# Encoder layer on one core: constant tables of the mixers loaded and split later, and the first k-tiles of the first gate block loaded singly

## The chip, the core and the metric

The kernel runs on one core of a Trainium2 chip. The metric is device time in microseconds (us). TensorE (PE in the rows) does the matmuls, ScalarE (ACT) and VectorE (DVE) the elementwise work, SyncE (SP) issues nearly all loads, and GpSimd (POOL) issues a few loads that add on the way.

## The reference

One layer, 256 tokens of 2048 numbers, all in fp32 (norms and rotations cut):

```
h = x + 0.5 * rms(swiglu(rms(x, g1)), p1)                 # first feed-forward step
u = rms(h, g);  q, k, v, f, g = split(u @ w_in)           # 16 query heads, 4 key/value heads
y_attn = gqa(rotate(rms(q)), rotate(rms(k)), v) @ w_attn_o
y_four = real(fft2(f, axes=(positions, 128 channels of a group))) @ w_fourier
h = h + rms((sigmoid(gA + bA) * y_attn + sigmoid(gB + bB) * y_four) @ w_out, p)
y = h + 0.5 * rms(swiglu(rms(h, g2)), p2)                 # second feed-forward step
```

## The kernel before

Each fp32 product is three matmuls of rounded numbers (`mm3`, L110 to L112): high part by high part, the same left side by the low part, low part by high part. `split` (L104, L105) makes the parts: ACT copies a tile into the high part (`whi`, `uh`), DVE subtracts that from the tile to get the low part (`wlo`, `ul`). In the rows `whi`, `wlo` are parts of weights, `raw` is the weight tile as loaded. Weights come through SP in 512 KB loads of two k-tiles into a ring of five raw tiles, and their parts go into a ring of six. `wk` is a pool of eight small tiles, `xpool` one of three larger ones. One 512-column `mm3` for each of the two token tiles and each of 16 k-tiles makes a block of 512 output columns (`col_block`, matmuls named `pc`).

Program order on each engine comes from a scheduler that keeps to dependences and resources; `tc.issue_after(x)` adds that an instruction stands behind x on its engine, and `latest["V"]` is the DVE instruction of the last `split`. `last_rows` is an exception: there DVE's order is written out by hand.

The places that the steps below touch, in order of time:

- `gate0` (L776 to L791): the first gate block of the first feed-forward step. For k-tiles 0 and 1 one weight tile (256 KB) and one tile of the input (`xt`, 128.5 KB) each, after that pairs (512 KB, 257 KB). `uh` (L786) and `ul` are the scaled input's parts.
- The end of the first feed-forward step and the start of the mixers (`last_rows`): DVE adds the normed result to h (L405), multiplies h by the next norm's gain (y, L418), and TensorE turns that (`pt`, L180) for the next input's parts. The constants' loads and splits are written at the start of the mixers: gains `gq`, `gk`, rotation tables `rc`, `rsn`, then the six tables of the discrete Fourier transform: `dps`, `dcs` (with low parts), `odd`, `first`, `alt`, `mid` (high part alone); their raw tiles are named `draw` and `mraw`.
- Gates 10 to 13 with `fold_f` between: the Fourier branch's product with its weight tile `fraw`, whose matmuls are named `pe`. `turn_k` transposes keys (`kT`) in gate 12.
- Gate 6 (j=0 of the attention loop) with `fourier_positions` (`pa`; `zh`, `zl` are the parts of `zs`; `al`, `ol` the low parts of its results, L973ff) and `fourier_channels` (`pb`, L1003ff) between its k-tiles.
- `fourier_weights(cb)` (L1107 to L1128): for each of four pieces of `w_fo` one load, two DVE steps in place (L1118, L1119), a `split`, and an accumulation (`acc`, L1126, L1128). `fourier_out(cb)` (L1133ff) uses them, in matmuls named `pf`; it is written behind the gate and `attn_scores` (`sc`, row maximum `mx`, exponentials `p`).

Of the kernel before, what the change touches and what calls it, by code (L numbers as in the profile page):

```python
# [2 lines left out]

# [1 line left out]

# [5 lines left out]
F32 = mybir.dt.float32  # L11
F32R = mybir.dt.float32r
BF16 = mybir.dt.bfloat16
I32 = mybir.dt.int32
AF = mybir.ActivationFunctionType
# [3 lines left out]
P = 128  # L19
# [39 lines left out]
def encoder_layer(  # L59
# [24 lines left out]
    def load(dst, src):  # L84
        nc.sync.dma_start(dst, src)
# [4 lines left out]
    def work(name, shape=None):  # L90
        return wk.tile(shape or [P, NB], F32, tag="wk", name=name)
# [11 lines left out]
    def split(hi, lo, src):  # L103
        a = A.activation(hi, src, AF.Copy)  # L104
        v = V.tensor_tensor(out=lo, in0=src, in1=hi.bitcast(F32), op=ALU.subtract)  # L105
        latest["A"], latest["V"] = a.ins, v.ins
# [83 lines left out]
    def col_block(u, w, nb, between=(), at=()):  # L190


        at = list(at)
        ps = [pmm.tile([P, NB], F32, tag="mm", name="pc") for _ in range(NT)]
        step = KD / (len(between) + 1)
        done = 0
        for kg in range(KD // CK):
            wt = weights(w[nb, kg])
            for k in range(CK):
                kk = kg * CK + k  # L200
                while at and kk >= at[0][0]:
                    with tc.issue_after(mm.ins):
                        at.pop(0)[1]()
                if done < len(between) and kk >= (done + 1) * step:
                    if between[done]:
                        with tc.issue_after(mm.ins):
                            between[done]()
                    done += 1
                for t in range(NT):
                    mm = mm3(ps[t][:], u[t][0][:, kk, :], u[t][1][:, kk, :], *wt[k], kk == 0, kk == KD - 1)  # L210
        return ps
# [563 lines left out]

    def gate0():  # L776
        ps = [pmm.tile([P, NB], F32, tag="mm", name="pc") for _ in range(NT)]
        for kk, n in [(0, 1), (1, 1)] + [(k, 2) for k in range(2, KD, 2)]:
            wt = piece(f1_gate[0, kk // CK], kk % CK, n)
            xt = xpool.tile([P, 2, S + 1], F32, tag="xt", name="xt")[:, 0:n, :]  # L780
            load(xt, xgT[:, kk:kk + n, :])
            xv = xt[:, :, 0:S].rearrange("p k (t c) -> p k t c", t=NT)
            for k in range(n):
                for t in range(NT):
                    uh, ul = u[t][0][:, kk + k, :], u[t][1][:, kk + k, :]
                    A.activation(uh, xv[:, k, t, :], AF.Copy, scale=xt[:, k, S:S + 1])  # L786
                    V.scalar_tensor_tensor(out=ul, in0=xv[:, k, t, :], scalar=xt[:, k, S:S + 1],
                                           in1=uh.bitcast(F32), op0=ALU.mult, op1=ALU.subtract)
                    mm3(ps[t][:], uh, ul, *wt[k], kk + k == 0, kk + k == KD - 1)
            if kk == 8:  # L790
                load(ident[:], ident_in)  # L791
        return ps
# [28 lines left out]
        load(spill[t], h[t][:])  # L821

    gq, gk = work("gq", [P, HD]), work("gk", [P, HD])
    load(gq[:], q_g.partition_broadcast(P))
    load(gk[:], k_g.partition_broadcast(P))
    rc, rsn = work("rc", [P, NT, HD]), work("rsn", [P, NT, HD])
    load(rc[:], rope_cos)
    load(rsn[:], rope_sin)
    tabs = {}

    def tables():
        for nm, g in (("q", gq), ("k", gk)):
# [59 lines left out]
        ts = slice(t * P, (t + 1) * P)  # L892
        transpose4(kro[t], kT[:, 0, :, ts], kT[:, 1, :, ts])

    def constant(src, n):
        raw = work("draw", [P, n])
        load(raw[:], src)
        return raw

    WE, WO = P + 2, P  # L900
    dps = const.tile([P, 2, WE + WO], F32R, name="dps")
    split(dps[:, 0, :], dps[:, 1, :], constant(dft_pos, WE + WO)[:])
    dcs = const.tile([P, 2, 2 * P], F32R, name="dcs")
    split(dcs[:, 0, :], dcs[:, 1, :], constant(dft_ch, 2 * P)[:])
    odd = const.tile([P, WE], F32R, name="odd")
    A.activation(odd[:], constant(dft_ones[:, 0:WE], WE)[:], AF.Copy)
    first = const.tile([P, P], F32R, name="first")
    A.activation(first[:], constant(dft_ones[:, WE:WE + P], P)[:], AF.Copy)
    alt = xpool.tile([P, GROUPS // 2, NYR], F32R, tag="xt", name="alt")
    A.activation(alt[:].rearrange("p a b -> p (a b)"), constant(dft_ones[:, WE + P:], GROUPS // 2 * NYR)[:], AF.Copy)  # L910
    mid = xpool.tile([NS, 2 * P + 2 * NYR], F32R, tag="xt", name="mid")
    mraw = work("mraw", [NS, 2 * P + 2 * NYR])
    load(mraw[:], dft_mid)
    A.activation(mid[:], mraw[:], AF.Copy)


    fs, fraw = [], {}
# [80 lines left out]
    def fourier_channels(b, i, a):  # L998

        (ah, al), (oh, ol) = a  # L1000
        j = 2 * b + i
        if j == 0:
            foT.append(new_chunk("foT"))
            pmid[0] = ptr.tile([P, NB], F32, tag="tr", name="pn")
        pb = ptr.tile([P, NB], F32, tag="tr", name="pb")
        c = slice(i * WO, (i + 1) * WO)
        mm3(pb[:, 0:WO], dcs[0:PO, 0, P:2 * P], dcs[0:PO, 1, P:2 * P], oh[0:PO, c], ol[0:PO, c], True, True)
        c, m, o = slice(i * WE, (i + 1) * WE), slice(2 * WE, 3 * WE), pb[:, WO:WO + WE]
        mm3(o, dcs[0:PO, 0, 0:P], dcs[0:PO, 1, 0:P], ah[0:PO, c], al[0:PO, c], True, False)
        T.matmul(o, mid[:, i * P:(i + 1) * P], ah[0:NS, m], start=False, stop=False)  # L1010
        T.matmul(o, mid[:, i * P:(i + 1) * P], al[0:NS, m], start=False, stop=True)
        o = pmid[0][0:NYR, 0:WE]
        T.matmul(o, alt[0:PO, j, :], ah[0:PO, c], start=j == 0, stop=False)
        T.matmul(o, alt[0:PO, j, :], al[0:PO, c], start=False, stop=False)
        if i == 1:
            n = slice(2 * P + b * NYR, 2 * P + (b + 1) * NYR)
            T.matmul(o, mid[:, n], ah[0:NS, m], start=False, stop=False)
            T.matmul(o, mid[:, n], al[0:NS, m], start=False, stop=b == 1)
        split(foT[0][0][:, j, :], foT[0][1][:, j, :], pb[:, 0:2 * P])
        A.activation(dcol[:, j:j + 1], pb[:, 2 * P:2 * P + 1], AF.Copy)  # L1020
        if j == 3:
            A.activation(mids[0:NYR, :], pmid[0][0:NYR, 0:P], AF.Copy)
            V.tensor_tensor(out=mids[64:NYR, :], in0=pmid[0][64:NYR, 0:P], in1=mids[64:NYR, :].bitcast(F32), op=ALU.subtract)
            A.activation(dcol[0:GROUPS, 4:5], pmid[0][0:GROUPS, P:P + 1], AF.Copy)
# [81 lines left out]
    def fourier_weights(cb):  # L1106


        acc = xpool.tile([P, NB], F32, tag="xt", name="acc")
        nraw, wn = xpool.tile([P, NB], F32, tag="xt", name="nraw"), workr("wn")  # L1110
        load(nraw[0:NYR, :], w_fn[cb])
        A.activation(wn[0:NYR, :], nraw[0:NYR, :], AF.Copy)
        V.tensor_tensor(out=wn[32:40, :], in0=nraw[32:40, :], in1=wn[32:40, :].bitcast(F32), op=ALU.subtract)
        forms = []
        for j in range(4):
            raw = wraw.tile([P, 2, NB], F32, tag="raw", name="raw")
            load(raw[:], w_fo[cb, j].rearrange("p (k c) -> p k c", k=2))
            V.tensor_tensor(out=raw[:, 0, :], in0=raw[:, 0, :], in1=raw[:, 1, :], op=ALU.add)  # L1118
            V.scalar_tensor_tensor(out=raw[:, 1, :], in0=raw[:, 1, :], scalar=-2.0, in1=raw[:, 0, :],  # L1119
                                   op0=ALU.mult, op1=ALU.add)  # L1120
            hi = wring.tile([P, 2, NB], F32R, tag="hi", name="whi")
            lo = wring.tile([P, 2, NB], F32R, tag="lo", name="wlo")
            split(hi[:], lo[:], raw[:])
            forms.append((hi, lo))
            if j == 0:
                V.tensor_scalar(out=acc[:], in0=raw[:, 0, :], scalar1=dcol[:, j:j + 1], scalar2=None, op0=ALU.mult)  # L1126
            else:
                V.scalar_tensor_tensor(out=acc[:], in0=raw[:, 0, :], scalar=dcol[:, j:j + 1], in1=acc[:],  # L1128
                                       op0=ALU.mult, op1=ALU.add)
        ready[cb] = acc, nraw, wn, forms  # L1130
# [21 lines left out]
            V.tensor_tensor(out=cbs(mB[t], cb), in0=w[:], in1=cbs(mB[t], cb), op=ALU.mult)  # L1152


    pv = col_block(u, w_in, 5, between=[nxt.finish, tables, lambda: fold_tokens(0)])
    for t in range(NT):
        vt = work("vt")
        A.activation(vt[:], pv[t][:], AF.Copy, scale=rs[t][:, 0:1])
# [7 lines left out]
    pq = col_block(u, w_in, 0, at=folds_at(4))  # L1166
    qs = []
    gate(11, mB, 1, at=folds_at(4), between=[lambda t=t: qs.append(norm_rope(pq, "q", t)) for t in range(NT)])
    gate(12, mB, 2, at=folds_at(4), between=[lambda t=t: turn_k(t) for t in range(NT)])
    gate(13, mB, 3, at=folds_at(4))  # L1170

    yA, zA = ([big(f"{n}{t}") for t in range(NT)] for n in ("yA", "zA"))
    mT = []
# [210 lines left out]
```

## Time and profile before

| | us |
|---|---|
| median of 3 runs (lowest, highest) | 2004.93 (2003.99, 2006.01) |
| profiled execution | 2006.3 |
| its span, first to last instruction | 2004.2 |
| TensorE busy, of that span | 1984.0 |
| VectorE busy | 1780.1 |
| ScalarE busy | 1301.2 |

The profiled execution has its own time beside its span: 2.1 us lie around the span, and the execution is 1.4 us above the median. Times in the rows are counted from the span's start. The mean granted TensorE clock is 0.997 of full speed.

### The profile page before, as it was taken

Reading aid. Unit: us, or ns where it says so; the run is one execution under the profiler, and the core shown is the slowest. Engines: PE = TensorE matmul, PEld = TensorE weight load, DVE = VectorE, ACT = ScalarE, POOL = GpSimd, SP = SyncE. Lnnn points to the kernel's source line nnn. Section 1 sums busy time; section 2 is a strip of 40 time slices with the busy share of each in tenths; the row PEclk is TensorE's granted clock in tenths of the full one; section 3 lists DMA queues with packets and bytes.
Section 4 is the critical chain, followed back from the end, with each engine's and each line's share of the span. In section 5 each row is a group of like instructions: output and inputs, shape, how many; then the busy total and the mean of one; then the engine's idle time right before and its main releaser. Section 6 shows DMA issues by size and latency. Waiting matters only on the chain.

```text
span 2004.2 us, 25805 instructions
## 1 busy us (share of the span) xinstructions
PE 1984.0 (99%) x9146; PEld 1644.8 (82%) x9146; DVE 1780.1 (89%) x2352; ACT 1301.2 (65%) x1860; POOL 84.5 (4%) x94
## 2 busy tenths in 40 slices
PE   9999999999999999999999999999999999999998
PEld 7888888888888878888888888878888888888886
DVE  6899999999999878886877885878999999999996
ACT  7566766767667756556666564656677766677666
POOL 0000000000000000100000000000000000000002
PEclk9999999999999999999999999999999999999999
DMA  8657766677668796954555557565577766677673
GB/s 319 211 175 240 225 232 199 200 249 228 226 204 275 250 280 201 261 184 138 195 189 188 192 166 277 194 215 194 169 236 231 231 210 208 213 233 229 208 264 126
DMA packets 117585, 434.20 MB, mean 217 GB/s; under 512 B 12840, under 2 KB 18992, under 8 KB 106064
## 3 DMA queue, kind: packets, MB, share of 16 engines
q1 hardware_dynamic: 103888, 411.65, 59.9%
q0 software_dynamic: 13568, 20.91, 6.0%
q8 instruction: 71, 1.16, 0.2%
q14 instruction: 58, 0.48, 0.1%
HBM read 409.44 MB, written 6.29 MB: 207 GB/s over the span
## 4 chain that ended last, share of the span: by engine, by line
PE 90%; DVE 5%; DMA 3%; ACT 1%; issue 1%; SPq 0%; DVEq 0%; ACTq 0%
PE pc L111 18%; PE pc L112 18%; PE pc L110 18%; PE pr L112 10%; PE pr L111 10%; PE pr L110 10%; DVE wlo L105 2%; PE pt L180 1%; DMA raw<-in_f_gu 1%; DMA raw<-in_w_fo 1%; DVE t L582 0%; PE pe L110 0%; PE pe L112 0%; PE pe L111 0%; PE pt L1072 0%
## 5 line engine op out<-in xcount | busy, mean ns | idle before, releaser
L105 DVE TENSOR_TENSOR wlo<-raw,whi 128x1024 fp32r<-128x1024 f32 (+1 forms) x567 | 681.1, 1219 | 96.9 <-ACT whi L104 95.2
L104 ACT ACTIVATE whi<-raw 128x1024 fp32r<-128x1024 f32 (+1 forms) x567 | 585.8, 1052 | 253.7 <-PE pc L112 109.3
L111 PE MATMUL pc<-wlo,fh 128*128 128x512 f32 x738 | 287.3, 389 | 0.0
L112 PE MATMUL pc<-whi,fl 128*128 128x512 f32 x738 | 287.3, 389 | 0.0
L110 PE MATMUL pc<-whi,fh 128*128 128x512 f32 x738 | 287.1, 389 | 0.0
L110 PE MATMUL pc<-whi,uh 128*128 128x512 f32 x688 | 271.7, 395 | 1.5 <-ACT uh L786 1.5
L111 PE MATMUL pc<-wlo,uh 128*128 128x512 f32 x688 | 269.8, 392 | 1.7 <-DVE wlo L105 1.7
L112 PE MATMUL pc<-whi,ul 128*128 128x512 f32 x688 | 269.6, 392 | 0.0
L104 ACT ACTIVATE whi<-t 128x1024 fp32r<-128x1024 f32 (+1 forms) x198 | 171.6, 867 | 139.4 <-DVE t L582 130.8
L582 DVE TENSOR_TENSOR t<-raw 128x512 f32<-128x512 f32 (+1 forms) x252 | 209.1, 842 | 14.1 <-DMA raw<-in_f_gu 10.3
L110 PE MATMUL pr<-whi,hTh 128*128 128x512 f32 x544 | 213.4, 392 | 0.0
L112 PE MATMUL pr<-whi,hTl 128*128 128x512 f32 x544 | 211.8, 389 | 0.0
L111 PE MATMUL pr<-wlo,hTh 128*128 128x512 f32 x544 | 211.7, 389 | 0.0
L105 DVE TENSOR_TENSOR wlo<-t,whi 128x1024 fp32r<-128x1024 f32 (+1 forms) x198 | 193.6, 978 | 13.4 <-ACT whi L104 13.0
L104 ACT ACTIVATE w<-raw 128x1024 fp32r<-128x1024 f32 x144 | 152.0, 1055 | 40.8 <-DVE raw L582 34.7
L105 DVE TENSOR_TENSOR w<-raw,w 128x1024 fp32r<-128x1024 f32 x144 | 175.6, 1219 | 0.0
L111 PEld LDWEIGHTS pc<-wlo,fh 128*128 128x128 f32 x738 | 138.5, 188 | 29.2 <-DVE wlo L105 0.3
L110 PEld LDWEIGHTS pc<-whi,fh 128*128 128x128 f32 x738 | 138.5, 188 | 28.9
L112 PEld LDWEIGHTS pc<-whi,fl 128*128 128x128 f32 x738 | 138.5, 188 | 28.7
L111 PEld LDWEIGHTS pc<-wlo,uh 128*128 128x128 f32 x688 | 129.8, 189 | 28.5 <-DVE wlo L105 3.6
L110 PEld LDWEIGHTS pc<-whi,uh 128*128 128x128 f32 x688 | 129.7, 188 | 28.5 <-ACT uh L786 2.8
L112 PEld LDWEIGHTS pc<-whi,ul 128*128 128x128 f32 x688 | 129.6, 188 | 27.0
(360 smaller groups left out, 3188.4 us busy)
## 6 DMA issues: line engine op xcount, KB each, us to landing
raw<-in_f_down SPq DMA_DIRECT2D x176, 512.0 KB, 5.0
raw<-in_f_gu SPq DMA_DIRECT2D x144, 512.0 KB, 4.8
raw<-in_f_gu SPq DMA_DIRECT2D x72, 1024.0 KB, 7.0
raw<-in_w_in SPq DMA_DIRECT2D x112, 512.0 KB, 4.5
raw<-in_f_up SPq DMA_DIRECT2D x32, 512.0 KB, 4.5
raw<-in_w_ao SPq DMA_DIRECT2D x32, 512.0 KB, 3.8
raw<-in_w_out SPq DMA_DIRECT2D x32, 512.0 KB, 4.5
raw<-in_f_gate SPq DMA_DIRECT2D x31, 512.0 KB, 5.8
```

The source lines that it names most:

```text
L104: a = A.activation(hi, src, AF.Copy)
L105: v = V.tensor_tensor(out=lo, in0=src, in1=hi.bitcast(F32), op=ALU.subtract)
L110: T.matmul(ps, lh, rh, start=first, stop=False, skip_group_check=onto)
L111: T.matmul(ps, lh, rl, start=False, stop=False, skip_group_check=onto)
L112: return T.matmul(ps, ll, rh, start=False, stop=last, skip_group_check=onto)
L180: T.transpose(pt[:, j, :], src[:, j * P:(j + 1) * P], ident[:])
L582: V.tensor_tensor(out=out, in0=a, in1=b, op=ALU.subtract)
```

## The change

Four edits. (1) In `gate0` the first `CK` = 4 k-tiles come singly, instead of the first two, and their input tiles move from `xpool` to `wk`. (2) The loads of `gq`, `gk`, `rc`, `rsn` become a step `rotation`, done between the k-tiles of the first column block of the mixers, and `tables`, which uses them, goes from the second slot to the fifth. (3) The six tables' loads (`ask`) and splits (`take`) go into gates 12 and 13. (4) In `fourier_weights` the first add of the first piece is put behind the last `split` on DVE.

```diff
     def gate0():
-        for kk, n in [(0, 1), (1, 1)] + [(k, 2) for k in range(2, KD, 2)]:
+        for kk, n in [(k, 1) for k in range(CK)] + [(k, 2) for k in range(CK, KD, 2)]:
             wt = piece(f1_gate[0, kk // CK], kk % CK, n)
-            xt = xpool.tile([P, 2, S + 1], F32, tag="xt", name="xt")[:, 0:n, :]
+            xt = work("xt", [P, 1, S + 1])[:] if n == 1 else xpool.tile([P, 2, S + 1], F32, tag="xt", name="xt")[:]
...
-    load(gq[:], q_g.partition_broadcast(P))
-    load(gk[:], k_g.partition_broadcast(P))
-    load(rc[:], rope_cos)
-    load(rsn[:], rope_sin)
+    def rotation():
+        load(gq[:], q_g.partition_broadcast(P))
+        load(gk[:], k_g.partition_broadcast(P))
+        load(rc[:], rope_cos)
+        load(rsn[:], rope_sin)
...
-    split(dps[:, 0, :], dps[:, 1, :], constant(dft_pos, WE + WO)[:])
-    split(dcs[:, 0, :], dcs[:, 1, :], constant(dft_ch, 2 * P)[:])
-    A.activation(odd[:], constant(dft_ones[:, 0:WE], WE)[:], AF.Copy)
-    A.activation(first[:], constant(dft_ones[:, WE:WE + P], P)[:], AF.Copy)
-    A.activation(alt[:].rearrange("p a b -> p (a b)"), constant(dft_ones[:, WE + P:], GROUPS // 2 * NYR)[:], AF.Copy)
-    load(mraw[:], dft_mid)
-    A.activation(mid[:], mraw[:], AF.Copy)
+    def ask(*names):
+        for n in names:
+            raw = work("draw", list(srcs[n].shape))
+            load(raw[:], srcs[n])
+            late[n] = raw
+    def take(*names):
+        for n in names:
+            raw = late[n]
+            if n in ("dps", "dcs"):
+                dst = {"dps": dps, "dcs": dcs}[n]
+                split(dst[:, 0, :], dst[:, 1, :], raw[:])
+            elif n in ("odd", "first"):
+                A.activation({"odd": odd, "first": first}[n][:], raw[:], AF.Copy)
...
     def fourier_weights(cb):
-            V.tensor_tensor(out=raw[:, 0, :], in0=raw[:, 0, :], in1=raw[:, 1, :], op=ALU.add)
+            with tc.issue_after(latest["V"]) if cb == 0 and j == 0 else nullcontext():
+                V.tensor_tensor(out=raw[:, 0, :], in0=raw[:, 0, :], in1=raw[:, 1, :], op=ALU.add)
...
-    pv = col_block(u, w_in, 5, between=[nxt.finish, tables, lambda: fold_tokens(0)])
+    pv = col_block(u, w_in, 5, between=[nxt.finish, rotation, lambda: fold_tokens(0), None, tables])
...
-    gate(12, mB, 2, at=folds_at(4), between=[lambda t=t: turn_k(t) for t in range(NT)])
-    gate(13, mB, 3, at=folds_at(4))
+    gate(12, mB, 2, at=folds_at(4), between=[lambda t=t: turn_k(t) for t in range(NT)]
+         + [lambda: ask("alt", "mid", "first"), None, lambda: take("alt", "mid", "first")])
+    gate(13, mB, 3, at=folds_at(4), between=[lambda: ask("dps", "odd", "dcs"), None, lambda: take("dps", "odd", "dcs")])
```

How it moves instructions, at three places; lines of the changed kernel are some 2 to 14 higher for the same text.

DVE at the start of the mixers (`h` L405, `y` L418: the step before the transposes), before:

```order
740 L105 TENSOR_TENSOR wlo<-raw,whi 128x1024
741 L405 SCALAR_TENSOR_TENSOR h_5676<-y_942,cr,h_5676 128x512
742 L105 TENSOR_TENSOR dps<-draw,dps 128x258
743 L418 TENSOR_TENSOR y_942<-h_5676,gpre_5722 128x512
744 L105 TENSOR_TENSOR wlo<-raw,whi 128x1024
745 L105 TENSOR_TENSOR dcs<-draw,dcs 128x256
```

and of the change:

```order
741 L105 TENSOR_TENSOR wlo<-raw,whi 128x1024
742 L405 SCALAR_TENSOR_TENSOR h_5684<-y_950,cr,h_5684 128x512
743 L439 TENSOR_REDUCE tot<-ssn 128x1
744 L418 TENSOR_TENSOR y_950<-h_5684,gpre_5730 128x512
745 L105 TENSOR_TENSOR wlo<-raw,whi 128x1024
746 L105 TENSOR_TENSOR ul_6374<-pt,uh_6373 128x512
```

The low parts of the two tables are gone from between h, y and wlo, and a small reduction stands there.

ACT in gate 12 (`alt`, `mid`, `first` are tables; `fraw` the fold's weights), before:

```order
615 L104 ACTIVATE whi<-fraw 128x1024
616 L104 ACTIVATE whi<-raw 128x1024 x2
617 L104 ACTIVATE whi<-fraw 128x1024
618 L104 ACTIVATE whi<-raw 128x1024 x2
619 L104 ACTIVATE kT<-pt 128x4x128
```

and of the change:

```order
611 L104 ACTIVATE whi<-fraw 128x1024
612 L924 ACTIVATE alt<-draw 128x288
613 L927 ACTIVATE mid<-draw 8x400
614 L104 ACTIVATE whi<-raw 128x1024
615 L921 ACTIVATE first<-draw 128x128
616 L104 ACTIVATE whi<-raw 128x1024
617 L104 ACTIVATE kT<-pt 128x4x128
618 L104 ACTIVATE whi<-fraw 128x1024
```

Three tables now stand ahead of and between the two weight copies, and `kT` ahead of the next `fraw`.

DVE from the last low row of gate 6 to the first maximum of the attention, where `fourier_weights` and `fourier_out` meet. Before, the L1118 and L1119 steps of all four pieces stood further up, among the positions (the first one right ahead of `zl`), and here:

```order
988 L1101 SCALAR_TENSOR_TENSOR z<-pc,r0r,bg 128x512
989 L1101 SCALAR_TENSOR_TENSOR z<-pc,r1r,bg 128x512
990 L1051 TENSOR_REDUCE mx<-sc 128x2
991 L105 TENSOR_TENSOR wlo<-raw,whi 128x1024
992 L1113 TENSOR_TENSOR wn<-nraw,wn 8x512
```

and of the change (L1132 and L1133 are the two steps, L1140 and L1142 the accumulations):

```order
975 L1114 SCALAR_TENSOR_TENSOR z<-pc,r0r,bg 128x512
976 L1114 SCALAR_TENSOR_TENSOR z<-pc,r1r,bg 128x512
977 L1126 TENSOR_TENSOR wn<-nraw,wn 8x512
978 L1132 TENSOR_TENSOR raw<-raw 128x512
979 L1064 TENSOR_REDUCE mx<-sc 128x2
980 L1133 SCALAR_TENSOR_TENSOR raw<-raw 128x512
981 L1140 TENSOR_SCALAR acc<-raw,dcol 128x512
982 L1065 TENSOR_SCALAR nmx<-mx 128x2
983 L1142 SCALAR_TENSOR_TENSOR acc<-raw,dcol,acc 128x512
984 L105 TENSOR_TENSOR wlo<-raw,whi 128x1024 x3
```

The first piece's two steps, all four pieces' low parts and the accumulations have moved to behind the gate's last rows; on ACT the four pieces' copies have moved likewise, to between the gate's sigmoids and the exponentials' table load.

## Rows read from the trace of the kernel before

**Rows 1.** The page's first and fourth part: busy time of each engine, and the chain of work that ended last, by engine.

```profile
PE 1984.0 (99%) x9146; PEld 1644.8 (82%) x9146; DVE 1780.1 (89%) x2352; ACT 1301.2 (65%) x1860; POOL 84.5 (4%) x94
...
PE 90%; DVE 5%; DMA 3%; ACT 1%; issue 1%; SPq 0%; DVEq 0%; ACTq 0%
```

**Rows 2.** The waits of TensorE, longest first: line, releaser, us in total, times, longest.

```profile
PE pt L180 <- DVE y L418: 2.5, 1, 2.5
PE pc L111 <- DVE wlo L105: 1.7, 4, 0.7
PE pa L979 <- DVE zl L105: 1.5, 1, 1.5
PE pc L110 <- ACT uh L786: 1.5, 2, 1.0
```

**Rows 3.** Instructions of TensorE at the program's start, in order of time: start, duration, what, idle time before and its releaser.

```profile
8.21 0.40 PE L112 MATMUL pc<-whi,ul 128*128 128x512 f32 x1
9.59 0.79 PE L110 MATMUL pc<-whi,uh 128*128 128x512 f32 x2 [0.98 <-ACT uh L786]
...
13.00 0.39 PE L110 MATMUL pc<-whi,uh 128*128 128x512 f32 x1
13.23 0.39 PE L111 MATMUL pc<-wlo,uh 128*128 128x512 f32 x1
```

**Rows 4.** The chain that ended last, at the program's start: start, us, what.

```profile
2.60 5.57 DMA raw<-in_f_gate
...
8.19 1.07 ACT whi L104
...
9.28 1.24 DVE wlo L105
```

**Rows 5.** The first loads by size (count, KB each, median us from issue to landing), and ACT's second half-size copy (from the instructions in order of time).

```profile
raw<-in_f_gate SPq DMA_DIRECT2D x2, 256.0 KB, 3.6
...
5.47 0.61 ACT L104 ACTIVATE whi<-raw 128x512 fp32r<-128x512 f32 x1
```

**Rows 6.** The start of the mixers: one row of the chain, then instructions of DVE and of TensorE in order of time.

```profile
705.85 6.88 DMA draw<-in_dft_pos
...
710.08 0.75 DVE L405 SCALAR_TENSOR_TENSOR h<-y,cr,h 128x512 f32<-128x512 f32 x1
713.20 0.43 DVE L105 TENSOR_TENSOR dps<-draw,dps 128x258 fp32r<-128x258 f32 x1 [2.38 <-ACT dps L104]
...
714.38 0.63 PE L180 MATMUL pt<-ident,y 128*128 128x128 f32 x4 [2.50 <-DVE y L418]
715.42 0.79 PE L111 MATMUL pc<-wlo,uh 128*128 128x512 f32 x1 [0.42 <-DVE wlo L105]
...
716.44 0.63 PE L110 MATMUL pc<-whi,uh 128*128 128x512 f32 x1
716.87 0.63 PE L111 MATMUL pc<-wlo,uh 128*128 128x512 f32 x1
```

**Rows 7.** Busy time of each engine in stretches of the span (PE, PEld, DVE, ACT, POOL, with the number of instructions), the mean granted clock (PEclk), DMA share, GB/s.

```profile
715.00:720.00 5.00, 4.58 (x17) 3.74 (x17) 4.10 (x8) 2.80 (x7) 0.00 (x0) 0.67 0.88 263
895.00:900.00 5.00, 4.94 (x25) 4.48 (x25) 4.93 (x10) 1.30 (x4) 0.00 (x0) 0.66 0.49 174
930.00:940.00 10.00, 10.00 (x48) 8.12 (x48) 7.07 (x14) 9.10 (x22) 0.00 (x0) 1.00 0.49 161
```

**Rows 8.** Gate 12: ACT's weight copies and TensorE's fold in order of time, and the 512 KB loads from 836 to 846 (median us to landing).

```profile
840.48 2.00 ACT L104 ACTIVATE whi<-raw 128x1024 fp32r<-128x1024 f32 x2
...
849.93 0.28 PE L111 MATMUL pe<-wlo,ueh 128*128 128x260 f32 x1
...
raw<-in_w_in SPq DMA_DIRECT2D x4, 512.0 KB, 5.3
```

**Rows 9.** Gate 6 with the Fourier positions: the chain's load, SP's third load of w_fo, then ACT, DVE and TensorE in order of time.

```profile
889.14 4.74 DMA raw<-in_w_fo
...
892.77 0.33 SPq L85 DMA_DIRECT2D raw<-in_w_fo  x1
...
892.43 0.41 ACT L104 ACTIVATE zh<-zs 128x260 fp32r<-128x260 f32 x1
...
893.98 0.69 DVE L1118 TENSOR_TENSOR raw<-raw 128x512 f32<-128x512 f32 x1 [1.23 <-DMA raw<-in_w_fo]
...
895.06 0.33 PE L979 MATMUL pa<-odd,zl 128*126 128x130 f32 x1 [1.51 <-DVE zl L105]
...
895.55 0.27 PE L978 MATMUL pa<-odd,zh 128*126 128x130 f32 x1
895.66 0.28 PE L979 MATMUL pa<-odd,zl 128*126 128x130 f32 x1
...
897.54 0.74 PE L110 MATMUL pc<-whi,uh 128*128 128x512 f32 x1
...
902.40 0.44 PE L110 MATMUL pc<-whi,uh 128*128 128x512 f32 x1
```

**Rows 10.** The end of gate 6: DVE's last row of the gate, then TensorE's first pf and the next block's first L111, in order of time.

```profile
927.90 0.74 DVE L1101 SCALAR_TENSOR_TENSOR z<-pc,r1r,bg 128x512 f32<-128x512 f32 x1
...
929.35 0.40 PE L110 MATMUL pf<-whi,foTh 128*128 128x512 f32 x1
...
936.14 0.39 PE L111 MATMUL pc<-wlo,uh 128*128 128x512 f32 x1
```

More of the change, by code (lines that the diff above doesn't have):

```diff
@@ L1 @@
 import math
-from contextlib import ExitStack
+from contextlib import ExitStack, nullcontext
 import numpy as np
@@ L893, in turn_k @@
         transpose4(kro[t], kT[:, 0, :, ts], kT[:, 1, :, ts])
[L895 to L898, printed above, removed]
     WE, WO = P + 2, P
     dps = const.tile([P, 2, WE + WO], F32R, name="dps")
-    split(dps[:, 0, :], dps[:, 1, :], constant(dft_pos, WE + WO)[:])
     dcs = const.tile([P, 2, 2 * P], F32R, name="dcs")
-    split(dcs[:, 0, :], dcs[:, 1, :], constant(dft_ch, 2 * P)[:])
     odd = const.tile([P, WE], F32R, name="odd")
-    A.activation(odd[:], constant(dft_ones[:, 0:WE], WE)[:], AF.Copy)
     first = const.tile([P, P], F32R, name="first")
-    A.activation(first[:], constant(dft_ones[:, WE:WE + P], P)[:], AF.Copy)
-    alt = xpool.tile([P, GROUPS // 2, NYR], F32R, tag="xt", name="alt")
-    A.activation(alt[:].rearrange("p a b -> p (a b)"), constant(dft_ones[:, WE + P:], GROUPS // 2 * NYR)[:], AF.Copy)
-    mid = xpool.tile([NS, 2 * P + 2 * NYR], F32R, tag="xt", name="mid")
-    mraw = work("mraw", [NS, 2 * P + 2 * NYR])
-    load(mraw[:], dft_mid)
-    A.activation(mid[:], mraw[:], AF.Copy)
+    late = {}
+    def ask(*names):
+        srcs = {"dps": dft_pos, "dcs": dft_ch, "odd": dft_ones[:, 0:WE], "first": dft_ones[:, WE:WE + P],
+                "alt": dft_ones[:, WE + P:], "mid": dft_mid}
+        for n in names:
[10 more added lines that the diff above has]
+                A.activation({"odd": odd, "first": first}[n][:], raw[:], AF.Copy)
+            elif n == "alt":
+                late[n] = xpool.tile([P, GROUPS // 2, NYR], F32R, tag="xt", name="alt")
+                A.activation(late[n][:].rearrange("p a b -> p (a b)"), raw[:], AF.Copy)
+            else:
+                late[n] = xpool.tile([NS, 2 * P + 2 * NYR], F32R, tag="xt", name="mid")
+                A.activation(late[n][:], raw[:], AF.Copy)
     fs, fraw = [], {}
@@ L1009, in fourier_channels @@
         mm3(o, dcs[0:PO, 0, 0:P], dcs[0:PO, 1, 0:P], ah[0:PO, c], al[0:PO, c], True, False)
-        T.matmul(o, mid[:, i * P:(i + 1) * P], ah[0:NS, m], start=False, stop=False)
-        T.matmul(o, mid[:, i * P:(i + 1) * P], al[0:NS, m], start=False, stop=True)
+        T.matmul(o, late["mid"][:, i * P:(i + 1) * P], ah[0:NS, m], start=False, stop=False)
+        T.matmul(o, late["mid"][:, i * P:(i + 1) * P], al[0:NS, m], start=False, stop=True)
         o = pmid[0][0:NYR, 0:WE]
-        T.matmul(o, alt[0:PO, j, :], ah[0:PO, c], start=j == 0, stop=False)
-        T.matmul(o, alt[0:PO, j, :], al[0:PO, c], start=False, stop=False)
+        T.matmul(o, late["alt"][0:PO, j, :], ah[0:PO, c], start=j == 0, stop=False)
+        T.matmul(o, late["alt"][0:PO, j, :], al[0:PO, c], start=False, stop=False)
         if i == 1:
             n = slice(2 * P + b * NYR, 2 * P + (b + 1) * NYR)
-            T.matmul(o, mid[:, n], ah[0:NS, m], start=False, stop=False)
-            T.matmul(o, mid[:, n], al[0:NS, m], start=False, stop=b == 1)
+            T.matmul(o, late["mid"][:, n], ah[0:NS, m], start=False, stop=False)
+            T.matmul(o, late["mid"][:, n], al[0:NS, m], start=False, stop=b == 1)
         split(foT[0][0][:, j, :], foT[0][1][:, j, :], pb[:, 0:2 * P])
```

## The prediction, made before the changed kernel ran

> **What bounds the kernel now.** I read the page's busy times first, then the chain that ended last [rows 1]: TensorE is busy for 1984.0 of 2004.2 us, and 90% of the chain is its own. Nothing off TensorE shortens this program except by taking away one of its few waits. The list of waits names them [rows 2]; all are small, and the change touches the places of the first, third and fourth. So I read each place in order of time, in the lists of TensorE, ScalarE (ACT), VectorE (DVE) and SyncE (SP, the loading queue), and ask what is late there before and what is late next. The clock matters too: after the waits at the mixers' start and at the Fourier positions the windows show a mean granted clock of 0.67 and 0.66 [rows 7], part of the stretch being at 1.2 GHz, and 512-column matmuls stand 0.43 us apart there instead of 0.23. After the wait at the start (0.98) it stayed at 2.4 GHz: the next ones stand 0.23 apart [rows 3].
>
> **Place 1, start of gate0.** Before, k-tiles 2 and 3 come as one pair: issued at 2.60, landed 5.57 later, copied for 1.07, subtracted for 1.24 [rows 4]. TensorE, through with k=1 at 8.44 (last start 8.21 plus its 0.23 spacing), starts k=2 at 9.59 and k=4 at 13.00 [rows 3]. Without the gap k=4 would start at 8.44 + 12 x 0.23 = 11.2: at most 1.8 is to be had. Now k=2 and k=3 come as 256 KB loads, which took 3.6 [rows 5]; issued at 2.6 and 3.55 they land by about 6.5 and 7.5, and their half-size splits (0.61 for the copy, [rows 5], and about as much for the low part) are done before 8.44. Late next is the pair k=4, 5: SP issues it some 0.95 later than now (two extra issues), and with the bytes ahead of it unchanged it lands at about 9.5 to 10. Plus 1.06 and 1.24, its low half is there at 11.8 to 12.3, where TensorE wants it at 11.2 + 2 x 0.23 = 11.7. So 0.1 to 0.6 of the 1.8 stays. I take **a gain of 1.2** (0.5 to 1.8).
>
> The Trainium skill speaks against this edit ("DMA: Bandwidth & Descriptors", section "Measured (HBM→SBUF, 128 partitions, SWDGE, issued from GpSimd)"): batch transfers to 1 MiB or more. By its fit (section "Anatomy of one DMA") of 2.0 us plus bytes over 436 GB/s, an estimate from that page is 3.2 for one pair and 5.2 for two halves one after the other, 2.0 later: place 1 would lose instead of gain. Here the rows show loads that overlap: the two 256 KB loads at the start were issued 0.92 apart (0.74 and 1.66), and the second was copied from 5.47 without a wait, 3.81 after its issue [rows 5]; one after the other they would have taken 7.2.
>
> **Place 2, start of the mixers.** Before, DVE's next step of the chain, the y of L418, stood behind the low half of dps, which waited for its table: issued at 705.85, landed after 6.88, DVE idle for 2.38 until 713.20 [rows 6]. TensorE lost 2.50 to that y, then 0.42 to a wlo, and ran the next matmuls at 0.43 [rows 6]. Afterwards no table stands there: DVE goes from h (710.08, 0.75) to a 0.15 reduction, y (0.69, taken from the add of L1118, [rows 9]; to 711.6) and wlo (to 712.7). TensorE, free from 711.7, does its four transposes with hardly a wait and has L111 at 712.76 instead of 715.42: 2.66. The six half-speed matmuls that followed cost 6 x (0.43 - 0.23) = 1.2, plus 0.15 in the transposes; with a wait of 0.5 left I expect full clock. **Gain 4.0** (3.0 if the clock still falls after the 0.7 wait for a wlo just before it, [rows 2], to 4.2). The gain loads and rotation tables now stand behind the second spill; the tables step that needs them runs three slots later in the same column block. SP's queue is the same length, so I cost that at nothing; were they late, the first norm would wait, as place 3 does.
>
> **Place 3, gate 12.** New here: ACT has alt and mid, which wait for DMA, ahead of two weight copies. Before, those copies ran from 840.48 without a wait [rows 8]. The tables are issued at about 837.9 behind two 512 KB loads that took 5.3 [rows 8], so they land at about 843.0. ACT stands still from 840.5, then alt 0.36, mid 0.42, copy 0.97, first 0.27, copy 0.97: 846.0. DVE's second wlo ends at 847.3, fraw's fold 847.9, ACT's copy of fraw 849.0, its wlo 850.2; TensorE wants it at 849.93 [rows 8]. **Cost 0.3**. Ends: 0 for a landing 0.3 sooner; for a landing as late as the 6.88 of dft_pos [rows 6] (844.8) 2.1, with a fall of the clock 3.6. Gate 13's three tables have no such queue of loads ahead; I cost them at nothing, with the one to two weight pieces that TensorE holds in store as the cover; without it they cost what gate 12's do.
>
> **Place 4, Fourier positions.** Before, DVE took w_fo's piece j=0 first and waited for it (4.74 from its issue at 889.14, DVE at 893.98), so zl came late and TensorE lost 1.51 [rows 9]; then half speed: the 17 matmuls from 895.06 took 2.48 to 897.54, and the next gate matmuls four at 0.43 [rows 9], until the channels' end at 902.40. Now j=0's add stands behind zl (pinned), and zl follows zh (892.43 + 0.41) and the wlo: done at 893.3. L979 starts at 893.4, 17 x 0.11 (895.55 to 895.66, [rows 9]) end at 895.3, twelve gate matmuls at 898.0. But the pin holds j=0 alone: j=1 and j=2 now stand ahead of al and ol, and j=2, issued at 892.77 [rows 9], lands at about 897.3 by 4.5. Then al 897.9, ol 899.5: TensorE waits 1.4 and has the channels (1.26) through at 900.7, not 902.4. **Gain 1.8** (0.2 if the 1.4 brings half speed as the 1.51 did, up to 3.1 if j=2 lands at 895.7).
>
> **Place 5, fourier_out(0): the price.** What was held back is late here. Before, all four w_fo pieces were split while the gate still ran; pf started at 929.35 without a wait and the next gate's L111 at 936.14 [rows 10]. Now DVE has the gate's last rows until 928.55 [rows 10], wn to 929.2, add to 929.8, mx to 930.4 and the second w_fo step to 931.1 (0.61 apart, an estimate from the 0.69 of L1118, [rows 9], of which the pipelining hides some). Only then ACT copies j=0: 931.1 to 932.15. TensorE waits 2.8 for its first pf. wlo of j=0 is there at 933.4, another 0.8. ACT has all four copies ahead of its table load and the exponentials, and DVE four wlo (1.14 each), four accumulations (0.69 or a little more, as [rows 9]), a maximum and the last low row ahead of the gate's wlo: 931.1 + about 9.8 = 940.9, where TensorE wanted it at 936.14. It has one L110 (0.23) done by then: **cost 4.5**. This contains the 2.8 and the 0.8, and a fall of the clock runs inside the wait before 940.9. Ends: 3.6 (only the first two waits count) and 6.5 (the fall on top, 1.9).
>
> **Sum:** -1.2 - 4.0 + 0.3 - 1.8 + 4.5 = -2.2. Against the profiled execution's 2006.3 that is 2004.1; that execution stands 1.37 above the median of 2004.93, so against the median it is **2002.7 us**. About 0.2%, 4.0 us, is what a measurement of this kernel can tell from no change.
>
> **Rivals.**
> - *Faster*: place 5 costs only its first two waits, 3.6, because DVE places its work in the gaps of ACT, and places 2 and 4 give all: -1.8 - 4.2 - 3.1 + 3.6 = -5.5, 1999.4. For it: TensorE's waits in the list are short wherever it has store. Against: the order holds nine wlo and accumulations ahead of the gate's. Chance 0.25.
> - *Slower*: gate 12's tables come late. The point from which it decides is a landing after 842.7; at 844.8 the fold waits 2.1 and the clock falls, 1.5 more. With place 4 at its low end: -1.2 - 4.0 + 3.6 - 0.2 + 4.5 = +2.7, 2007.6. For it: dft_pos took 6.88 behind other loads. Against: only 1 MB is ahead here. 0.11.
> - *ACT becomes the bound in the exponentials*: it is busy for 9.10 of 10 us after 930 already [rows 7]; four copies of 0.97 more exceed the stretch by 3.0. On top of 4.5 that is 7.5: 2005.7. Against: in order, DVE ends later than ACT. 0.09.
> - *The small loads pay in turn*: with 3.6 each after the second, k=2 lands at 9.1 and k=3 at 12.7; k=3 then runs from 14.0 on and k=4 from 15.4, 2.4 later than now: 2002.7 + 1.2 + 2.4 = 2006.3. 0.04. The Trainium skill's page named above has such a sum.
>
> **How the numbers follow.** The forecast has 0.51, its own range 2000.9 to 2005.0. The rest is above. Range **1998.8 to 2007.8**: it reaches below the faster rival and above the slower one, and leaves out some 0.1 on each side (places 2 to 5 all at one end). Faster by over 0.2% (under 2000.9): 0.25 of the first rival and 0.03 of the forecast's tail. Slower by over 0.2% (over 2008.9): 0.10, from the second and third rival together. The same: 0.62.
>
> **What would show it.** Right, if the waits no longer list y L418, the 0.98 for uh is gone, and a new wait of some 3 us for ACT's copy at pf (after's L110, by 930) stands with 0.8 and about 1 for wlo. Wrong, if pf starts without a wait (place 5 too dear: then 1998 to 1999), if the fold of gate 12 waits over 1 us, or if L979's wait stays.

## The result: slower by 0.24%, and the profile after

The changed kernel took 2010.72 us (median of 9 runs, 2008.20 to 2012.83) beside 2006.65 for the kernel before on the same chip: ratio 1.0024, 95% interval 1.0015 to 1.0032, so +4.8 us (3.0 to 6.4; the two medians differ by 4.1). The forecast was 2.2 us faster, and the range, whose upper end is 2007.8, is missed on its slow side.

The span of the profiled execution went from 2004.2 to 2007.7 us. The waits of TensorE, to be held against [rows 2] (line, releaser, total us, times, longest):

```profile
PE pf L110 <- ACT whi L104: 2.9, 1, 2.9
PE pc L111 <- DVE wlo L105: 2.0, 4, 1.0
PE pe L111 <- DVE wlo L105: 2.0, 3, 0.9
PE pt L180 <- DVE o L869: 2.0, 1, 2.0
...
PE pb L110 <- ACT oh L104: 1.1, 1, 1.1
PE pc L110 <- ACT uh L786: 0.6, 1, 0.6
PE pf L111 <- DVE wlo L105: 0.3, 1, 0.3
```

The waits for y, for zl and most of that for uh are gone, as forecast, and pf's wait is there. Two rows stand here that the forecast did not have as they are: three waits of the folds (`pe`), of which it had one, at 0.3, and a wait for `o` (the rotation in the next block, 0.4 before).

The list of waits leaves out what half speed costs. So for each stretch I summed how much later each of TensorE's matmuls started than full clock allows (0.2285 us after a 512-column one, 0.12 after 252 to 260, 0.11 after 128 or 130), from the instructions in order of time. One trace each, us lost by this count:

| stretch | before | changed | forecast | measured |
|---|---|---|---|---|
| start, to k-tile 5 | 4.36 | 4.45 | -1.2 | +0.1 |
| start of the mixers | 5.88 | 2.78 | -4.0 | -3.1 |
| folds of gates 11, 12, 13 | 0.25 + 0 + 0 | 0.49 + 1.50 + 1.64 | +0.3 | +3.4 |
| positions and channels | 4.59 | 3.26 | -1.8 | -1.3 |
| fourier_out(0) | 0 | 5.13 | +4.5 | +5.1 |
| turn of q at 988 | 0.64 | 2.12 | 0 | +1.5 |

These add to +5.7. The span grew by 3.5: 1.0 came back in the second feed-forward step (last section), 0.8 between 1010 and 1485, where the trace of before is 0.6 to 0.9 longer than every other trace here, and the small rest is spread over places that also differ from run to run.

**The folds**, beside [rows 8]. ACT, DVE and TensorE of the changed kernel in gates 12 and 13, in order of time for each engine:

```profile
841.83 0.45 ACT L924 ACTIVATE alt<-draw 128x288 fp32r<-128x288 f32 x1 [3.96 <-DMA draw<-in_dft_ones]
...
870.91 0.42 ACT L104 ACTIVATE dps<-draw 128x258 fp32r<-128x258 f32 x1 [3.39 <-DMA draw<-in_dft_pos]
...
843.68 2.38 DVE L105 TENSOR_TENSOR wlo<-raw,whi 128x1024 fp32r<-128x1024 f32 x2 [3.88 <-ACT whi L104]
845.97 0.68 DVE L954 SCALAR_TENSOR_TENSOR fraw<-fraw 128x504 f32<-128x504 f32 x1
...
847.83 1.23 DVE L105 TENSOR_TENSOR wlo<-fraw,whi 128x1024 fp32r<-128x1024 f32 x1 [0.58 <-ACT whi L104]
...
847.85 0.39 PE L110 MATMUL pe<-whi,ueh 128*128 128x260 f32 x1
849.11 0.38 PE L111 MATMUL pe<-wlo,ueh 128*128 128x260 f32 x1 [0.87 <-DVE wlo L105]
...
878.28 0.39 PE L111 MATMUL pe<-wlo,ueh 128*128 128x260 f32 x1 [0.88 <-DVE wlo L105]
```

ACT stands still for 3.96 us, DVE behind it for 3.88, then the chain runs as I had it: two low parts, fraw's step (L954), its copy, its low part, TensorE. It happens again in gate 13, where I had put nothing: TensorE waits 0.87 in gate 12 and 0.88 in gate 13 for the fold's low part.

**The mixers' start**, beside [rows 6]: DVE and TensorE.

```profile
710.99 0.75 DVE L405 SCALAR_TENSOR_TENSOR h<-y,cr,h 128x512 f32<-128x512 f32 x1
711.65 0.15 DVE L439 TENSOR_REDUCE tot<-ssn 128x1 f32<-128x4 f32 x1
711.77 0.70 DVE L418 TENSOR_TENSOR y<-h,gpre 128x512 f32<-128x512 f32 x1
...
712.64 0.60 PE L180 MATMUL pt<-ident,y 128*128 128x128 f32 x4
713.65 0.50 PE L111 MATMUL pc<-wlo,uh 128*128 128x512 f32 x1 [0.41 <-DVE wlo L105]
```

y follows h at once. The 0.42 wait of before stands as 0.41, and the clock stays (1.00 in 715 to 720, where [rows 7] has 0.67).

**fourier_out(0)**, beside [rows 10]: DVE, ACT and TensorE, then the window.

```profile
929.52 0.68 DVE L1133 SCALAR_TENSOR_TENSOR raw<-raw 128x512 f32<-128x512 f32 x1
...
930.24 3.90 ACT L104 ACTIVATE whi<-raw 128x1024 fp32r<-128x1024 f32 x4 [2.01 <-DVE raw L1133]
...
931.35 0.94 PE L110 MATMUL pf<-whi,foTh 128*128 128x512 f32 x2 [2.91 <-ACT whi L104]
932.61 0.79 PE L111 MATMUL pf<-wlo,foTh 128*128 128x512 f32 x1 [0.31 <-DVE wlo L105]
933.20 0.63 PE L112 MATMUL pf<-whi,foTl 128*128 128x512 f32 x1
933.63 0.63 PE L111 MATMUL pf<-wlo,foTh 128*128 128x512 f32 x1
...
930.00:940.00 10.00, 8.34 (x32) 6.44 (x33) 10.00 (x16) 9.73 (x18) 0.00 (x0) 0.83 0.56 186
```

The first wait is 2.91 where I had 2.8. After it the matmuls stand 0.43 apart (933.20 to 933.63), and DVE is busy for all ten microseconds.

### The profile page after: what moved, and what is told of

It is laid out like the page before. It is cut to its first block, busy times and chain, and to the rows that moved or that the text cites. A ratio compares the mean times of both kernels' runs of the same rounds, so it can differ in the third digit from the quotient of the medians.

```text
span 2007.7 us, 25813 instructions
## 1 busy us (share of the span) xinstructions
PE 1983.9 (99%) x9146; PEld 1643.3 (82%) x9146; DVE 1779.0 (89%) x2353; ACT 1300.0 (65%) x1861; POOL 84.4 (4%) x94
## 4 chain that ended last, share of the span: by engine, by line
PE 91%; DVE 5%; DMA 2%; ACT 1%; issue 1%; SPq 0%; DVEq 0%; ACTq 0%
PE pc L111 18%; PE pc L112 18%; PE pc L110 18%; PE pr L112 10%; PE pr L111 10%; PE pr L110 10%; DVE wlo L105 2%; PE pt L180 1%; DMA raw<-in_w_fo 1%; ACT whi L104 0%; DMA raw<-in_f_gu 0%; PE pe L111 0%; PE pf L111 0%; PE pe L112 0%; PE pf L112 0%
## 5 line engine op out<-in xcount | busy, mean ns | idle before, releaser
L111 PE MATMUL pc<-wlo,fh 128*128 128x512 f32 x738 | 287.1, 389 | 0.0
L111 PE MATMUL pc<-wlo,uh 128*128 128x512 f32 x688 | 269.2, 392 | 2.0 <-DVE wlo L105 2.0
L111 PE MATMUL pr<-wlo,hTh 128*128 128x512 f32 x544 | 211.7, 389 | 0.0
L111 PEld LDWEIGHTS pc<-wlo,fh 128*128 128x128 f32 x738 | 138.5, 188 | 28.8
L111 PEld LDWEIGHTS pc<-wlo,uh 128*128 128x128 f32 x688 | 129.5, 188 | 28.8 <-DVE wlo L105 3.7
```

What stands on the lines that cost most here:

```text
L111: T.matmul(ps, lh, rl, start=False, stop=False, skip_group_check=onto)
```

## The experiments

Twelve kernels, each timed in five rounds beside the kernel before on its chip; differences in us are the ratio times 2005.

| run | ratio to before, 95% interval | us |
|---|---|---|
| e1_pin_alone | 1.0032 (1.0020 to 1.0044) | +6.4 |
| e2_tables_alone | 0.9994 (0.9985 to 1.0003) | -1.2 |
| e3_singles_alone | 0.9995 (0.9986 to 1.0003) | -1.0 |
| e4_no_pin | 0.9991 (0.9982 to 1.0000) | -1.8 |
| e5_take_behind | 0.9973 (0.9963 to 0.9982) | -5.4 |
| e6_zl_pin | 0.9996 (0.9987 to 1.0005) | -0.8 |
| e7_take_behind_zl_pin | 0.9975 (0.9966 to 0.9984) | -5.0 |
| e8_singles_six | 0.9999 (0.9990 to 1.0007) | -0.2 |
| e9_after_take_behind | 1.0006 (0.9997 to 1.0015) | +1.2 |
| e10_ol_pin_alone | 0.9987 (0.9978 to 0.9996) | -2.6 |
| e11_take_behind_ol_pin | 0.9963 (0.9951 to 0.9976) | -7.4 |
| e12_take_behind_ol_pin_six | 0.9970 (0.9959 to 0.9982) | -6.0 |

### Which edit costs: each alone, and all but the pin

My theory (A): the fourth edit, the pin, is the price, at the place that I had named. The rival (B): the late tables leave a backlog on ACT and DVE, and that makes the loss in fourier_out. The first kernel has the fourth edit alone, the second kernel the second and third together, the third the first alone, and the fourth is the change without the pin:

```diff
 # e4_no_pin, against the changed kernel
-            with tc.issue_after(latest["V"]) if cb == 0 and j == 0 else nullcontext():
-                V.tensor_tensor(out=raw[:, 0, :], in0=raw[:, 0, :], in1=raw[:, 1, :], op=ALU.add)
+            V.tensor_tensor(out=raw[:, 0, :], in0=raw[:, 0, :], in1=raw[:, 1, :], op=ALU.add)
```

> The kernel before with the fourth edit alone (the first w_fo add held behind the last split). Theory A, the pin is the price: since the last split at that point of the program is the last one of gate 6, the splits of all four pieces move behind the gate; positions and channels lose 1.3 us less than before, the first pf waits about 3 and fourier_out loses 5.1 in all, the rotation before the wait at 987 loses 1.5 more: +5.3 us, between +4 and +6. Theory B, the backlog that the late tables leave on ACT and DVE makes the loss in fourier_out: then the pin alone gives 0 to +1 and no wait at pf over 1 us.

> The kernel before with the second and third edit alone (rotation and Fourier tables asked for and split later). Theory A: 3.1 us gained at the start of the mixers, about 3.6 lost in three folds of gates 11 to 13 because ACT stands still for the tables (3.96 and 3.39 us): 0 to +1 us, and nothing new at 929. Theory B: +3 to +4, with a wait at pf.

> The kernel before with the first edit alone (four k-tiles loaded singly). Theory A: the wait for the pair 2, 3 goes to the pair 4, 5, which now lands later: 0 us, within 0.5. My forecast before the run: -1.2 us. The trace is to show the wait for uh at k-tile 4 and not at 2, and k-tile 5 starting within 0.3 us of before (14.36).

> The changed kernel without the fourth edit. Theory A: 5.3 us faster than the changed kernel, thus within 1.5 us of the kernel before; pf starts without a wait; L979 waits again for zl. Theory B: within 1 us of the changed kernel, so +3 to +5 against before.

Theory B falls. The pin alone gives +6.4, with 2.92 us of wait at pf though all tables are early there; without it (e4_no_pin) the change is at or below the time of before, and pf starts without a wait. TensorE's waits with the pin alone:

```profile
PE pt L180 <- DVE y L418: 3.2, 2, 2.8
PE pf L110 <- ACT whi L104: 2.9, 1, 2.9
...
PE pt L180 <- DVE o L867: 1.0, 1, 1.0
```

The wait for `o` grows with the pin: 1.0 here, 1.3 in e9_after_take_behind below and 2.0 in the changed kernel, beside 0.3 to 0.6 in the kernels without it. That the backlog which the pin leaves on DVE is the link was not tried apart. e2_tables_alone is a little faster than A had it; within its interval it is no change. Its trace gains 3.1 at the start of the mixers, and the folds of gates 12 and 13 take 3.2.

e3_singles_alone: no measurable gain (interval 2.8 us faster to 0.6 slower). Its trace loses 4.2 us at the start where before lost 4.36, its k-tile 5 starts at 14.20 where before has 14.36, and it shows where the wait went. ACT and TensorE of e3_singles_alone:

```profile
10.77 1.06 ACT L104 ACTIVATE whi<-raw 128x1024 fp32r<-128x1024 f32 x1 [1.22 <-DMA raw<-in_f_gate]
...
12.18 0.79 PE L110 MATMUL pc<-whi,uh 128*128 128x512 f32 x2 [0.69 <-ACT uh L786]
13.15 0.74 PE L111 MATMUL pc<-wlo,uh 128*128 128x512 f32 x2 [0.18 <-DVE wlo L105]
```

The wait at k-tile 2 (0.98, [rows 3]) is now 0.69 at k-tile 4, whose pair is copied at 10.77 and not at the 9.5 to 10 of my forecast.

### What the late tables cost: copies behind the next weight copies

```diff
 # e5_take_behind, against e4_no_pin
     def take(*names):
+        with tc.issue_after(latest["A"]):
+            copies(*names)
+
+    def copies(*names):
         for n in names:
```

`latest["A"]` is the last weight copy at that point of the program; ACT's order then has eight more weight and key copies ahead of `alt` and five more ahead of `dps`, and the loads stay where they were.

> The changed kernel without the fourth edit, and with the copies of the late tables put behind the last weight copy on ACT; their loads stay where they are. Theory A: the folds of gates 12 and 13 lost 3.2 us only because ACT stood still for tables that land 6.0 to 6.6 us after their issue; with four to six copies in between, 0 to 0.7 is left, ACT's waits for draw are under 0.5 each, and the kernel is 2.5 to 3 us faster than e4_no_pin: about -4.5 against before. Theory C, DVE and ACT are near their limit there and give back what the start of the mixers gained in any order: the folds still lose over 2 us, and the time is that of e4_no_pin within 1 us.

Confirmed: 3.6 us faster than e4_no_pin, a little more than expected (the intervals, 3.6 to 7.4 and 0 to 3.6 faster than before, just meet). ACT of e5_take_behind has no wait for either table,

```profile
849.19 0.43 ACT L927 ACTIVATE alt<-draw 128x288 fp32r<-128x288 f32 x1
...
871.14 0.40 ACT L104 ACTIVATE dps<-draw 128x258 fp32r<-128x258 f32 x1
```

and no fold waits for a low part. Theory C falls. The second question is whether the same edit mends the changed kernel with its pin:

> The changed kernel with all its edits, and the copies of the late tables put behind the last weight copy on ACT. If my third step (0.3 forecast, 3.6 read from the trace) is what carried the time out of the range, this is 3 to 4 us faster than the changed kernel: +1 to +2 us against before, pf still waiting about 3. If the pin's loss grows by what the folds no longer lose, it is within 1.5 us of the changed kernel.

It does, in part: +1.2 us (0.6 faster to 3.0 slower) where the changed kernel has +4.8 (3.0 to 6.4), at pf still 2.9 of wait. So some 3.6 us of the result are the late tables'; the intervals just meet, and the traces agree: the folds of gates 12 and 13, which lose 3.1 in the changed kernel, lose nothing in this one.

### The positions: where the w_fo steps should stand

```diff
 # e6_zl_pin, against e4_no_pin (e7_take_behind_zl_pin: against e5_take_behind)
         split(zh[:], zl[:], zs[b])
+        behind.setdefault("V", latest["V"])
...
+            with tc.issue_after(behind["V"]) if cb == 0 and j == 0 else nullcontext():
```

> The changed kernel with the first w_fo add held behind zl of the first positions, not behind the last split of gate 6. Theory A: the wait for zl (2.0 in e4_no_pin) is gone, pf starts without a wait as in e4_no_pin; al and ol come some 1 us later, as my fourth step had it: 1 to 2 us faster than e4_no_pin. Rival: the w_fo loads, for which DVE then waits behind zl, hold al and ol by as much as zl was held: 0 us.

> Both edits of e5_take_behind and e6_zl_pin together. Theory A: the gains add, 4 us faster than e4_no_pin and some 6 us (0.3%) faster than the kernel before. Theory C: at most 2 us faster than e4_no_pin.

The rival of e6_zl_pin is right: nothing is gained over e4_no_pin (the intervals overlap), and e7_take_behind_zl_pin is no faster than e5_take_behind. DVE and TensorE of e6_zl_pin:

```profile
892.62 0.43 DVE L105 TENSOR_TENSOR zl<-zs,zh 128x260 fp32r<-128x260 f32 x1
893.68 0.69 DVE L1134 TENSOR_TENSOR raw<-raw 128x512 f32<-128x512 f32 x1 [0.63 <-DMA raw<-in_w_fo]
...
899.27 0.40 DVE L105 TENSOR_TENSOR ol<-pa,oh 126x256 fp32r<-126x256 f32 x1
...
893.10 0.33 PE L994 MATMUL pa<-odd,zl 128*126 128x130 f32 x1
...
899.18 0.33 PE L110 MATMUL pb<-oh,dcs 126*128 126x128 f32 x1 [1.11 <-ACT oh L104]
899.73 0.33 PE L111 MATMUL pb<-ol,dcs 126*128 126x128 f32 x1 [0.23 <-DVE ol L105]
```

zl is on time, and six w_fo steps (L1134 and L1135) then stand ahead of ol: TensorE waits at the channels instead, and half speed follows there (granted clock 0.66 from 900 to 905). This is the wait that my fourth step had named. It can be taken away by holding all four pieces, and these behind ol; which of the two differences does it was not tried apart:

```diff
 # e10_ol_pin_alone, against the kernel before (e11_take_behind_ol_pin: against e5_take_behind)
         split(oh[0:PO, :], ol[0:PO, :], po[0:PO, 0:2 * WO])
+        behind.setdefault("V", latest["V"])
...
+            with tc.issue_after(behind["V"]) if cb == 0 else nullcontext():
```

> The kernel before with all four w_fo pieces of the first block held behind ol of the first positions, and nothing else changed. If the positions lose only because DVE stands at a w_fo load ahead of zl, al or ol, the waits at L979 and at pb are both gone and full clock stays: 2.5 to 3.5 us faster than before, pf without a wait. If DVE then has too little room until the end of gate 6, pf waits over 1 us and the gain is under 1 us.

> The kernel of e5_take_behind with the pin of e10_ol_pin_alone. Gains at different places should add: -5.4 and -3, thus 7 to 9 us (0.35 to 0.45%) faster than before, and the fastest so far. If half speed or a backlog gives one of them back: -5 to -6.

Both come as expected: -2.6 alone (interval -4.4 to -0.8), and -7.4 together with the late tables behind the copies. That is the lowest time of all and clearly faster than before and the change. Its interval, -9.8 to -4.8, overlaps those of e5, e7 and e12, and leaves the sum of -8 open by a microsecond or two. DVE of e10_ol_pin_alone has ol at 897.05, the first w_fo step without a wait behind it, and e11_take_behind_ol_pin has no wait of over 1.2 us left on TensorE:

```profile
897.05 0.43 DVE L105 TENSOR_TENSOR ol<-pa,oh 126x256 fp32r<-126x256 f32 x1
897.39 0.68 DVE L1121 TENSOR_TENSOR raw<-raw 128x512 f32<-128x512 f32 x1
```

```profile
PE pc L111 <- DVE wlo L105: 2.0, 4, 1.0
PE idle L772 <- DVE zero L769: 1.2, 1, 1.2
PE pe L110 <- ACT q L858: 1.2, 1, 1.2
PE pc L110 <- ACT uh L786: 0.9, 2, 0.7
PE pt L180 <- DVE o L869: 0.6, 1, 0.6
```

### The start: six k-tiles singly

```diff
 # e8_singles_six (and e12_take_behind_ol_pin_six), against e3_singles_alone (e11_take_behind_ol_pin)
-        for kk, n in [(k, 1) for k in range(CK)] + [(k, 2) for k in range(CK, KD, 2)]:
+        for kk, n in [(k, 1) for k in range(6)] + [(k, 2) for k in range(6, KD, 2)]:
```

> The kernel before with the first six k-tiles loaded singly. If the first loads are late because a pair lands late as a whole, the wait for uh moves on to k-tile 6 and shrinks: 0.5 us faster than e3_singles_alone (loss at the start 3.4 instead of 3.95 us). If the bytes are late, the loss at the start stays at 3.9 to 4.4 us and only its place moves.

> The kernel of e11_take_behind_ol_pin with the first six k-tiles loaded singly. The trace of e8_singles_six lost 3.3 us at the start, those of four single k-tiles 4.0 to 4.9, but its time was that of before: 0 to 1 us faster than e11_take_behind_ol_pin if the start's loss is what counts, 0 if it varies by as much from run to run.

Inconclusive on the mechanism. The trace of e8_singles_six loses 3.3 us at the start, as if the pair's landing counted, but e12_take_behind_ol_pin_six loses 4.4. That neither run's time is better than its partner's has a second reason, outside the start: the same 2644 matmuls between 100 and 690 us, where these kernels do not differ, take 591.3 us in both traces and 590.1 to 590.2 in eleven of the twelve others (590.9 in e2_tables_alone, with a wait of 0.5 there). So six single k-tiles cost 1.2 us far from the loads, by matmuls that stand a little further apart (last section), which is more than e8_singles_six gains at the start.

## Why the prediction was wrong

- **Place 3, the step that failed.** "Cost 0.3" in gate 12 and nothing in gate 13; measured 1.5 and 1.6, together 3.1, and some 3.6 by e9_after_take_behind against the changed kernel. The chain was right, down to the order of the links; two things were not. The landing: alt could be copied 6.6 us after its issue at 835.23, where I had reckoned 5.1; I had the 6.88 of dft_pos [rows 6] before me and kept it for the dear end and the rival. And the cover: in gate 13 I named the "one to two weight pieces that TensorE holds in store". The gate's matmuls did run on through ACT's stop without a wait, but the fold's copy does not come out of that store: it stands behind the blocked copies on ACT and its low part behind two others on DVE, and the fold waits for it. Had I costed both gates at gate 12's late end (2.1 each, without half speed), the sum would have been +1.7. The 0.49 in gate 11 is not the tables': e3_singles_alone, e8_singles_six and e10_ol_pin_alone, without those edits, lose 0.5 to 0.8 there, before loses 0.25, and e2, e4 and e5, with those edits, nothing.
- **Place 5.** 4.5 forecast, 5.1 in the changed kernel, 5.2 in e1_pin_alone. The first wait (2.91 for 2.8) was right; the composition of the rest was not, so that the size came out near is in part luck. The pieces' low parts did not hold up the gate's wlo (its L111 ran at 940.35 with no wait beside it), and half speed, which I had hidden inside that wait, was in the open. What I left out, a term of the sum that I put at nothing, is the 1.5 at the turn of q: DVE is full from 930 to 940, and the rotation behind it comes later; that it is this backlog which arrives there was not tried apart.
- **Place 2.** 4.0 forecast, 3.1 measured. The tables' removal did what I said, and full clock stayed. Of the 0.9 that I missed, 0.3 is h itself, which came later against the matmuls (a wait of 1.0 for a wlo just before it, 0.7 in [rows 2]), and 0.4 a late `ul` at 704. e1_pin_alone has both of these without the tables' edits, so they are not the change's.
- **Place 1.** 1.2 forecast, 0 measured in the changed kernel (k-tile 5 starts at 14.38, before at 14.36); e3_singles_alone bounds it to between 2.8 faster and 0.6 slower. The wait moved to the pair 4, 5, as I said it might, but that pair landed about 1 us later than I assumed. The Trainium skill's sum in "DMA: Bandwidth & Descriptors" (section "Anatomy of one DMA", which is on loads issued by GpSimd, while these go through SP) gives, as an estimate, a loss of 2.0 us; no run shows that loss, nor a gain.
- **Place 4.** 1.8 forecast, 1.3 measured, and in the way described, al and ol behind w_fo, with a wait of 1.1 where I had 1.4. That it gained at all is in part luck: e9_after_take_behind, with the same pin and the same two waits (1.09 and 0.23, here 1.06 and 0.23), fell to half speed behind them, lost 4.9 there and gained nothing over before; the low end of my range for this place, 0.2, had that case.
- **The rivals.** The slower one had the right mechanism, late tables in gate 12, and the right sign, at a chance of 0.11; it did not count gate 13. That its 3.6 is near what the folds lost is luck: 1.5 of it was a fall of the clock, and the clock stayed (granted 1.00 from 849 to 854).

Of the errors, 2.8 are place 3's (gates 12 and 13), 1.5 the turn of q's, 1.3 place 1's, 0.9 place 2's, 0.6 place 5's and 0.5 place 4's, all to the same side. In places 1 and 3 it was the landing of a load that I took from the rows' better cases; the turn of q I had not looked at.

## What to carry to other kernels

Moving a load later, out of a busy moment, moves its wait to whichever in-order engine consumes it: cost every place where a copy stands behind a fresh load by issue-to-landing under the traffic there, and put the copy well behind the load in the consumer's order (here eight and five more copies were enough). A pin behind "the latest" instruction holds the work behind what is latest when that code is written down, here the end of the gate; name the instruction that must go first, and hold every piece of a set: in the changed kernel and in e6_zl_pin unpinned pieces stood ahead of al and ol. If an engine runs near full (DVE, 10.00 of 10 us), look further down for a second payment of a delay; here 1.5 us were lost 50 us later, a link that was not tried apart.

## What the runs showed of the hardware

Under load, small tables took as long as large ones here: tables of 64 to 144 KB were there 5.4 to 6.6 us after their issue in gates 12 and 13, 512 KB weight loads in the same stretches after 3.6 to 6.4.

After waits of 0.87 and 0.88 us the clock stayed at its upper level (2.4 GHz); after 2.91 it fell to the lower one (1.2 GHz). In between the same wait went both ways. TensorE at the channels with the granted clock of a window behind it (the third number from the end), first in the changed kernel, then in e9_after_take_behind:

```profile
899.88 0.33 PE L110 MATMUL pb<-oh,dcs 126*128 126x128 f32 x1 [1.06 <-ACT oh L104]
...
900.00:905.00 5.00, 4.77 (x27) 3.95 (x28) 3.57 (x7) 1.64 (x4) 0.00 (x0) 1.00 0.23 84
```

```profile
895.90 0.33 PE L110 MATMUL pb<-oh,dcs 126*128 126x128 f32 x1 [1.09 <-ACT oh L104]
...
896.00:901.00 5.00, 4.77 (x19) 3.78 (x20) 3.60 (x7) 1.66 (x4) 0.00 (x0) 0.71 0.22 74
```

Each of these is followed by a wait of 0.23. The changed kernel kept full clock and e9_after_take_behind did not; e6_zl_pin, with 1.11 and 0.23, did not either. So a gain that hangs on a wait of about 1.1 us staying cheap is not a safe one.

In the second feed-forward step (from about 1480 to 1950) 512-column matmuls stood 0.2267 or 0.2268 us apart on average in the eight kernels that hold the second and third edit and at most four single k-tiles, and 0.2272 to 0.2273 in the five without those two edits and in e12_take_behind_ol_pin_six, which has them and six single k-tiles. Between 100 and 700 us all have 0.2267 to 0.2268, except e8_singles_six and e12_take_behind_ol_pin_six with 0.2272. For the same 2054 matmuls of the second feed-forward step this is 460.1 us against 459.1 to 459.2, so the changed kernel gets 1.0 us back there. No run here shows its cause.
